# Order of weight preparation and evacuation at the start of both FFNs of a two-layer trunk

## The chip, the cores and the metric

The kernel runs on one core of a Trainium2 chip. The metric is the device time of one execution in microseconds (us). TensorE (PE in the profile, with PEld for its weight loads), VectorE (DVE), ScalarE (ACT) and GpSimd (POOL) each run their own queue in order; the sync engine (SP) issues most loads. An instruction that needs another engine's result waits for a semaphore, and everything behind it on its engine waits with it.

## The reference

Two layers, each a mixer with a residual and then a gated FFN with a residual, RMSNorm ahead of each, and a last RMSNorm. 512 tokens, 1024 channels, float32. The change is in the FFN, which stands once in each layer, with 2816 hidden channels:

```
def gated_conv_ffn(x, w_gate, w_up, conv_w, conv_b, w_down):
    g = jnp.einsum('bsd,df->bsf', x, w_gate)
    g = causal_dwconv3(g, conv_w) + conv_b
    up = jnp.einsum('bsd,df->bsf', x, w_up)
    return jnp.einsum('bsf,fd->bsd', jax.nn.silu(g) * up, w_down)
...
        hn = rms_norm(h, norm_ffn[layer])
        h = h + gated_conv_ffn(hn, w_ffn_gate[layer], w_ffn_up[layer], conv_ffn[layer],
                               b_conv_ffn[layer], w_ffn_down[layer])
```

## The kernel before, in words

Every float32 operand of a matmul is split into a high part (a rounded copy, made by ACT) and a low part (the rest, made by a DVE subtraction, or by an ACT copy with the sign turned and a GpSimd DMA that adds the original). A product is then three matmuls: high by high, high by low, low by high. Tiles named whi_ and wlo_ are the parts of weights, hgh and hgl those of the normalized input.

The 2816 hidden channels are 22 tiles of 128. `Ffn.steps` (L785) takes them in groups of two tiles, f = 0, 2, 4 and so on; in the text "group 2" is f = 2. For each group the gate (g) and up (u) projections are formed; then a `half_down` adds older groups' share of the down projection (PE rows named d in the first FFN and dn in the second), and `split_acts` splits the group's activations for it. A pool of 7 PSUM banks, "mm", carries all these products.

Group 0 is computed plainly by `direct` (L605), 96 matmuls of three passes into four banks gu_0 to gu_3. Its weights come from `pair_weights`. Its `evacuate` (L619) is the way out of the banks, for each of the two gate tiles: multiply by the norm's factor into a padded row (DVE, L624), convolve (`conv` L572: an ACT product, L575, then two DVE steps, L577, on a tile c), silu (ACT, L585, on a tile s, with a load of the function table ahead of the first), in the first FFN one more multiply by the norm's factor (DVE, L627), and then the product with the up bank (DVE, L630).

All later groups go through `both` (L682), a fast scheme with seven block products instead of eight for each of g and u. Its first half, up to L719, prepares weights: four loads of 512 KB into a pool of 4 raw tiles (`ffn_weights`, L547), the parts of the first blocks (tile a11), sums and differences of blocks on DVE (s12: L699, L701; s34: L710, L712), and their parts: whi_ on ACT and wlo_ on DVE (`halves`, L678), or for the blocks g and u themselves `summed` (L136: ACT L140, GpSimd DMA L141, ACT L143). Tiles of parts come from pools of 6 for each of high and low. Its second half runs the products in the order of the list at L745. Product numbers say which tiles take part: 1 uses a11, 5 and 6 use s12, 2 and 4 the blocks themselves, 7 and 3 use s34. Products 1, 6, 7 and 4 of one key add up in the same bank (PE rows g_2a, u_2a), 5 and 3 in another (g_2e, u_2e), 2 in a third (g_2b, u_2b). Between two products of a bank, ACT copies its state out (L733, to rows for g and to kept for u) or DVE adds it (L738, L743), so the next product of that bank waits for the copy.

The text's order is not the order on the engines. Except where `inorder` or `behind` pins an instruction, the framework's scheduler orders each engine's queue by its own estimate of readiness and by the order in which the text issues the instructions; tile buffers and semaphores follow from it. In the text before, the calls for groups 0 and 2 come in this order: direct products, block sums of the input (`block_sums`, L635), evacuation of group 0, preparation of group 2, products of group 2, half_down, split of the activations.

Of the kernel before, what the change touches and what calls it, by code (L numbers as in the profile page):

```python
# [32 lines left out]
def tile_trunk(ctx: ExitStack, tc: tile.TileContext, x, norm_mix, norm_ffn, final_norm,  # L33
# [50 lines left out]
    def behind(ins, first):  # L84

        if first is not None:
            tc.add_manual_dep(ins.ins, first.ins.name, mybir.DependencyInfo(
                mybir.DependencyClass.NoSync, mybir.DependencyReason.DATA), reason="order")
# [47 lines left out]
    def summed(raw, a, b, name, between=lambda: None):  # L136

        hi = wp.tile([P, a, b], F32R, tag="whi", bufs=6, name=f"whi_{name}")
        lo = wp.tile([P, a, b], F32R, tag="wlo", bufs=6, name=f"wlo_{name}")
        first = nc.scalar.activation(lo, raw, AF.Copy, scale=-1.0)  # L140
        nc.gpsimd.dma_start(lo, raw, accum_op=ALU.add)  # L141
        between()
        behind(nc.scalar.activation(hi, raw, AF.Copy), first)  # L143
        return hi, lo
# [138 lines left out]
    def padded_tile():  # L283
        turn[0] += 1
        return padded[turn[0] % NPADDED]
# [261 lines left out]
    def ffn_weights(layer, f, order):  # L547
        cs = slice(f * P, (f + 2) * P)
        return {(key, half): fetch(
            (w_ffn_gate if key == "g" else w_ffn_up)[layer][half * 512 : (half + 1) * 512, cs]  # L550
            .rearrange("(k p) c -> p k c", p=P), 4, 256, f"{key}{layer}_{f}_{half}")
            for key, half in order}

    class Ffn:
# [124 lines left out]
            nc.scalar.activation(hi, src, AF.Copy)  # L679
            nc.vector.tensor_tensor(lo, src, hi.bitcast(F32), ALU.subtract)  # L680

        def both(self, f):  # L682

            layer, ap, n = self.layer, self.ap, f"{self.layer}_{f}"
            raws = ffn_weights(layer, f, [(key, half) for half in range(2) for key in "gu"])
            stat = {}

            def put(key, product, hi_lo, i):
                stat[key, product] = hi_lo[0][:, i], hi_lo[1][:, i]

            w = self.unit(f"a11_{n}")
            for i, key in enumerate("gu"):
                self.halves(w[0][:, i], w[1][:, i], raws[key, 0][0][:, :, :P])
                put(key, 1, w, i)
            for key in "gu":
                r0, r1 = raws[key, 0][0], raws[key, 1][0]
                s12, s34 = (ap.tile([P, 2, 4, P], F32, tag="sum", bufs=3, name=f"{x}{key}_{n}")
                            for x in ("s12", "s34"))
                behind(nc.vector.tensor_tensor(s12[:, 0], r0[:, :, P:], r1[:, :, P:], ALU.add),  # L699
                       self.added[key])  # L700
                nc.vector.tensor_tensor(s12[:, 1], s12[:, 0], r0[:, :, :P], ALU.subtract)  # L701
                w = self.unit(f"s12{key}_{n}")

                def split_s12():
                    self.halves(*w, s12)

                hi, lo = summed(*raws[key, 1], between=split_s12)
                put(key, 5, w, 0)
                put(key, 6, w, 1)
                behind(nc.vector.tensor_tensor(s34[:, 0], r0[:, :, :P], r0[:, :, P:],  # L710
                                               ALU.subtract), self.added[key])
                nc.vector.tensor_tensor(s34[:, 1], r1[:, :, :P], s12[:, 1], ALU.subtract)  # L712
                for i, product in enumerate((2, 4)):
                    c = slice(i * P, (i + 1) * P)
                    stat[key, product] = hi[:, :, c], lo[:, :, c]
                w = self.unit(f"s34{key}_{n}")
                self.halves(*w, s34)
                put(key, 7, w, 0)
                put(key, 3, w, 1)  # L719

            banks = {"g": {}, "u": {}}
            kept = ap.tile([P, 3, HALF], F32, tag="kept", bufs=1, name=f"kept{n}")
            pads = [padded_tile() for _ in range(2)]
            lo, hi = slice(2, 2 + HALF), slice(2 + HALF, 2 + S)
            dst = {("g", 1): pads[0][:, lo], ("g", 6): pads[0][:, hi], ("g", 7): pads[1][:, hi],
                   ("g", 4): pads[1][:, lo]}
            dst.update({("u", product): kept[:, i, :] for i, product in enumerate((1, 6, 7))})
            onto = {2: 1, 5: 7, 3: 6}
            s, pending = {}, {}

            def after(key, product, ps):
                if (key, product) in dst:
                    nc.scalar.copy(dst[key, product], ps)  # L733
                elif product == 5 and (key, 7) not in pending:
                    pending[key, 5] = ps
                elif product in onto:
                    d = dst[key, onto[product]]
                    nc.vector.tensor_tensor(d, ps, d, ALU.add)  # L738
                if (key, product) == ("u", 4):
                    pending["u", 4] = ps  # L740
                if product == 7:
                    d = dst[key, 7]
                    self.added[key] = nc.vector.tensor_tensor(d, pending[key, 5], d, ALU.add)  # L743

            for key, product in (("g", 1), ("u", 1), ("g", 5), ("g", 6), ("u", 5), ("u", 6),  # L745
                                 ("g", 2), ("g", 7), ("u", 2), ("u", 7), ("g", 4), ("g", 3),
                                 ("u", 4), ("u", 3)):
                after(key, product, self.multiply(banks[key], f"{key}{n}", product,
                                                  stat[key, product]))
                if (key, product) in (("g", 4), ("g", 3)):  # L750
                    j = product == 4
                    row = pads[j][:, 2:]
                    nc.vector.tensor_tensor(row, row, self.r, ALU.mult)
                    s[j] = self.silu(self.conv(pads[j], f + j), f + j)
                    if j and layer == 0:
                        nc.vector.tensor_tensor(s[1], s[1], self.r, ALU.mult)
            nc.vector.tensor_tensor(s[1][:, HALF:], kept[:, 2, :], s[1][:, HALF:], ALU.mult)
            nc.vector.tensor_tensor(s[1][:, :HALF], pending["u", 4], s[1][:, :HALF], ALU.mult)
            if layer == 0:
                nc.vector.tensor_tensor(kept[:, :2, :], kept[:, :2, :],  # L760
                                        self.r.rearrange("p (a b) -> p a b", a=2), ALU.mult)
            s0 = s[0].rearrange("p (a b) -> p a b", a=2)
            nc.vector.tensor_tensor(s0, kept[:, :2, :], s0, ALU.mult)
            return [(f + 1, s[1]), (f, s[0])]

        def hidden(self, f, before=lambda i, j: None):

            if f == 0:
                def first(i, j):
                    before(i, j)  # L770
                    if (i, j) == (3, 0):
                        nc.vector.tensor_copy(self.cols, self.norm.rstd_cols(inorder))
                    elif (i, j) == (6, 0):
                        self.r = self.norm.rstd_spread(inorder)

                ch = self.pair_weights([("g", 0), ("u", 0), ("g", 1), ("u", 1)])
                rest = self.direct(ch, first)
                for kp in range(NP):
                    self.block_sums(kp)
                rows = rest()  # L780
            else:
                rows = self.both(f)
            return rows

        def steps(self, half_down, before=lambda i, j: None):  # L785

# [14 lines left out]
    def ffn0(norm):  # L801
        nonlocal prm1
        with tc.tile_pool(name="f0", bufs=1) as ap:
            def sums(kp):
                return [ap.tile([P, 2, HALF], F32R, name=f"t23{i}_{kp}") for i in "hl"]

            ffn = Ffn(0, prm0, norm, ap, sums)
            def half_down(a, b, half):
                project(f"d0_{a}", w_ffn_down[0], ffn.acts, list(range(a, b)), None,
                        halves=(half,), tail=0)  # L810

            ffn.split_acts(ffn.steps(half_down))
            prm1 = params1()
            nxt = Norm("m1", lambda k: prm1("mix", k))
            project("d0_last", w_ffn_down[0], ffn.acts, list(range(NF - 4, NF)), nxt)
            return nxt
# [370 lines left out]
    n = mixer0()  # L1187
    n = ffn0(n)
    n = mixer1(n)
# [31 lines left out]
```

## Time and profile before

| what | value |
|---|---|
| time before, median of 3 runs | 991.21 us (991.19 to 992.14) |
| the profiled execution's own time | 991.47 us |
| its span in the trace | 989.4 us |
| DVE busy | 770.3 us (78%) |
| ACT busy | 549.6 us (56%) |
| POOL busy | 101.0 us (10%) |
| read from memory | 98.42 MB, 102 GB/s over the span |
| granted TensorE clock | 0.999 of full speed |

How to read it: the trace starts all engines at the span's start. A row of the order of time gives the start, the length, the engine, the line of the kernel, the operation, the tiles written and read, and a count where equal rows follow each other. Brackets at the end hold the time that the engine had been idle and what ended that. Matmuls are pipelined: a matmul of 256 columns is shown 0.28 us long, while the next one starts 0.12 us after it, so an idle time in brackets is shorter than the delay of the start. On ACT and DVE, too, the next instruction starts a little before the shown end of the one before. The first FFN's products begin at 146.5 us and the second's at 632.6 us.

### The profile page before, as it was taken

To read this page: it belongs to the slowest core of one execution; us is meant where nothing else is said; L and a number is where in the kernel's file an instruction comes from. 1 tells how busy PE (TensorE), PEld (TensorE's weight loads), DVE (VectorE), ACT (ScalarE), POOL (GpSimd) and SP (SyncE) were. 2 spreads that over 40 slices of the span, in tenths; PEclk is the share of its full clock that TensorE was granted. 3 is DMA by queue.
4 is the path that set the end of the run, shared out by engine and by line. 5 is a ranking of instruction groups with operands and counts; after the bars stand their busy time and mean duration, and the time that the engine had idled before them with its cause. 6 is when DMAs were issued, how large, how long until landed. Compare 5 with 4: busy or idle time off the path is not lost.

```text
span 989.4 us, 15461 instructions
## 1 busy us (share of the span) xinstructions
PE 978.7 (99%) x6117; PEld 882.7 (89%) x6117; DVE 770.3 (78%) x1170; ACT 549.6 (56%) x823; POOL 101.0 (10%) x118
## 2 busy tenths in 40 slices
PE   9999999999999999999999999999999999999997
PEld 6788888899999999999889988889999999999986
DVE  5897458998788887886887665589987779777776
ACT  5623346765465654655487734676655456554544
POOL 2142022100000000000210001210000000000000
PEclk9999999999999999999999999999999999999999
DMA  7342225555455454553324623265555555455512
GB/s 247 131 149 85 86 86 128 131 143 153 129 149 133 131 142 129 150 129 110 124 64 116 199 74 102 54 139 129 150 162 134 131 148 146 118 136 135 143 49 85
DMA packets 86420, 125.64 MB, mean 127 GB/s; under 512 B 4196, under 2 KB 58188, under 8 KB 86348
## 3 DMA queue, kind: packets, MB, share of 16 engines
q1 hardware_dynamic: 77228, 98.24, 32.1%
q0 software_dynamic: 7200, 24.12, 13.4%
q10 hardware_dynamic: 1920, 2.30, 0.8%
q8 instruction: 48, 0.79, 0.3%
q14 instruction: 24, 0.20, 0.1%
HBM read 98.42 MB, written 2.10 MB: 102 GB/s over the span
## 4 chain that ended last, share of the span: by engine, by line
PE 85%; DVE 6%; ACT 3%; issue 1%; DMA 0%; ACTq 0%; POOL 0%; DVEq 0%
PE dn L154 4%; PE dn L155 4%; PE dn L156 4%; PE d L155 3%; PE d L154 3%; PE d L156 3%; PE oo L156 1%; PE oo L154 1%; PE oo L155 1%; PE oe L156 1%; PE oe L155 1%; PE oe L154 1%; PE u_20a L543 1%; PE u_18a L543 1%; PE u_16a L543 1%
## 5 line engine op out<-in xcount | busy, mean ns | idle before, releaser
L154 PE MATMUL dn<-whi_dn,a_hi 128*128 128x512 f32 (+1 forms) x180 | 69.3, 385 | 0.0
L155 PE MATMUL dn<-wlo_dn,a_hi 128*128 128x512 f32 (+1 forms) x180 | 69.3, 385 | 0.0
L156 PE MATMUL dn<-whi_dn,a_lo 128*128 128x512 f32 (+1 forms) x180 | 69.2, 384 | 0.0
L577 DVE SCALAR_TENSOR_TENSOR c<-rows,prm,c 128x512 f32<-128x512 f32 x88 | 63.8, 746 | 0.2 <-ACT c L575 0.2
L141 POOL DMA_DIRECT2D wlo_g<-raw_g x20 | 17.2, 861 | 385.2 <-ACT wlo_g L140 369.6
L154 PE MATMUL d<-a_hi,whi_d 128*128 128x512 f32 x144 | 56.1, 390 | 0.0
L155 PE MATMUL d<-a_lo,whi_d 128*128 128x512 f32 x144 | 56.1, 390 | 0.0
L156 PE MATMUL d<-a_hi,wlo_d 128*128 128x512 f32 x144 | 56.0, 389 | 0.0
L150 DVE TENSOR_TENSOR wlo_dn<-raw_dn,whi_dn 128x1024 fp32r<-128x1024 f32 x22 | 26.9, 1224 | 26.2 <-ACT whi_dn L149 26.0
L680 DVE TENSOR_TENSOR wlo_s34u<-s34u,whi_s34u 128x1024 fp32r<-128x1024 f32 x20 | 24.5, 1225 | 26.7 <-ACT whi_s34u L679 26.7
L1100 DVE SCALAR_TENSOR_TENSOR y<-dn,small,y 128x512 f32<-128x512 f32 (+1 forms) x49 | 33.9, 737 | 8.8 <-PE dn L156 8.8
L156 PEld LDWEIGHTS dn<-whi_dn,a_lo 128*128 128x128 f32 x180 | 33.8, 188 | 6.9 <-DVE a_lo L263 0.2
L154 PEld LDWEIGHTS dn<-whi_dn,a_hi 128*128 128x128 f32 x180 | 33.9, 188 | 6.5
L155 PEld LDWEIGHTS dn<-wlo_dn,a_hi 128*128 128x128 f32 x180 | 33.9, 188 | 6.3
L143 ACT ACTIVATE whi_u<-raw_u 128x1024 fp32r<-128x1024 f32 x21 | 22.1, 1055 | 30.0 <-PE d L155 16.3
L149 ACT ACTIVATE whi_dn<-raw_dn 128x1024 fp32r<-128x1024 f32 x22 | 23.3, 1059 | 25.5 <-issue 12.6
L261 ACT ACTIVATE a_hi<-s 128x512 fp32r<-128x512 f32 x44 | 27.4, 625 | 18.0 <-PE dn L155 12.3
L150 DVE TENSOR_TENSOR wlo_d<-raw_d,whi_d 128x1024 fp32r<-128x1024 f32 x18 | 22.0, 1224 | 19.7 <-ACT whi_d L149 19.7
L199 ACT ACTIVATE hgh<-h,prm 128x512 fp32r<-128x512 f32 x24 | 17.3, 723 | 35.1 <-DVE h L310 35.0
L585 ACT ACTIVATE s<-c,prm 128x512 f32<-128x512 f32 x44 | 31.2, 714 | 9.3 <-DVE c L577 9.3
L141 POOL DMA_DIRECT2D wlo_u<-raw_u x21 | 18.1, 862 | 166.4 <-ACT wlo_u L140 83.8
L210 POOL TENSOR_TENSOR ssq_f<-ssq_f,sq_f 128x512 f32<-128x512 f32 x14 | 19.8, 1412 | 131.2 <-ACT sq_f L209 96.3
(1435 smaller groups left out, 3664.0 us busy)
## 6 DMA issues: line engine op xcount, KB each, us to landing
raw_g<-in_w_ffn_gate_dram SPq DMA_DIRECT2D x40, 512.0 KB, 3.9
raw_u<-in_w_ffn_up_dram SPq DMA_DIRECT2D x40, 512.0 KB, 3.7
raw_dn<-in_w_ffn_down_dram SPq DMA_DIRECT2D x22, 512.0 KB, 3.6
wlo_u<-raw_u POOLq DMA_DIRECT2D x21, 512.0 KB, 5.6
wlo_g<-raw_g POOLq DMA_DIRECT2D x20, 512.0 KB, 4.7
raw_d<-in_w_ffn_down_dram SPq DMA_DIRECT2D x18, 512.0 KB, 3.7
raw_oe<-in_w_out_even_dram SPq DMA_DIRECT2D x8, 512.0 KB, 3.6
raw_v<-in_w_in_odd_dram SPq DMA_DIRECT2D x8, 512.0 KB, 4.6
```

The source lines that it names most:

```text
L141: nc.gpsimd.dma_start(lo, raw, accum_op=ALU.add)
L149: behind(nc.scalar.activation(hi, raw, AF.Copy), after[1])
L150: behind(nc.vector.tensor_tensor(lo, raw, hi.bitcast(F32), ALU.subtract), after[0])
L154: nc.tensor.matmul(ps, lhs[0], rhs[0], start=start, stop=False)
L155: nc.tensor.matmul(ps, lhs[0], rhs[1], start=False, stop=False)
L156: nc.tensor.matmul(ps, lhs[1], rhs[0], start=False, stop=stop)
L261: nc.scalar.activation(hi, src, AF.Copy, scale=scale)
L543: nc.tensor.matmul(ps, l, r, start=first, stop=end, skip_group_check=True)
L577: nc.vector.scalar_tensor_tensor(c, t[:, i : S + i], prm("cf", i * NF + ft), c, op0=ALU.mult, op1=ALU.add)
L585: nc.scalar.activation(s, c, AF.Silu, bias=self.prm("bf", ft))
L680: nc.vector.tensor_tensor(lo, src, hi.bitcast(F32), ALU.subtract)
L1100: nc.vector.scalar_tensor_tensor(dst, ps, ffn.cols[:, t : t + 1], dst, op0=ALU.mult, op1=ALU.add)
```

## The change

The method `both` is cut in two: `prepare`, which ends with the weight tiles in the dictionary `stat`, and `products`, which starts at the banks. For group 0 `hidden` now calls `prepare(2)` ahead of group 0's evacuation and keeps what it returns; for group 2 it uses that, and all later groups call both halves one after the other, as before. It applies to both layers' FFNs.

```diff
-        def both(self, f):
+        def prepare(self, f):
...
                 put(key, 7, w, 0)
                 put(key, 3, w, 1)
-
+            return stat
+
+        def products(self, f, stat):
+
+            layer, ap, n = self.layer, self.ap, f"{self.layer}_{f}"
             banks = {"g": {}, "u": {}}
...
                 for kp in range(NP):
                     self.block_sums(kp)
-                rows = rest()
-            else:
-                rows = self.both(f)
-            return rows
+                self.second = self.prepare(2)
+                return rest()
+            return self.products(f, self.second if f == 2 else self.prepare(f))
```

No instruction is added or left out; the text's order of the instructions named above is what differs, and with it the order that the scheduler gives them. Lines from L717 on are three or four further down in the changed kernel (L733 is L737 there, L738 is L742, L743 is L747).

## The prediction, made before the changed kernel ran

> **What bounds the kernel now.** First the page's head, then the busy time of the stretch between TensorE's first matmul (1.26 us) and its last (982.35 us):
>
> ```profile
> span 989.4 us, 15461 instructions
> PE 978.7 (99%) x6117; PEld 882.7 (89%) x6117; DVE 770.3 (78%) x1170; ACT 549.6 (56%) x823; POOL 101.0 (10%) x118
> ```
> ```profile
> 1.26:982.35 981.09, 978.74 (x6117) 882.71 (x6117) 767.54 (x1160) 548.23 (x819) 100.36 (x106) 1.00 0.47 128
> ```
>
> TensorE (PE) is busy 978.74 us of these 981.09: only 2.35 us can be won inside, and a little more where a matmul that had waited makes its follower late. The rest of the span (1.26 us ahead, 7.05 us behind) lies outside the change. So the second view is who PE waits for:
>
> ```profile
> PE u_2e L543 <- DVE wlo_s12u L680: 1.9, 2, 0.9
> PE g_2a L543 <- ACT rows L733: 0.2, 1, 0.2
> ```
>
> Nearly all of the 2.35 us is the second group (f = 2): two waits for the low part of the u sums (wlo_s12u), one in each FFN, and one for the copy of the first g product (rows, L733). The third view is PE's order of time there, in the first FFN and then in the second (start, length; in brackets the idle time before and what ended it):
>
> ```profile
> 174.00 0.40 PE L543 MATMUL u_2e<-t,whi_s12u 128*128 128x256 f32 x2
> 175.35 0.39 PE L543 MATMUL u_2e<-t,wlo_s12u 128*128 128x256 f32 x1 [0.95 <-DVE wlo_s12u L680]
> ...
> 177.37 0.28 PE L543 MATMUL g_2b<-hgh,whi_g 128*128 128x256 f32 x1
> 177.81 0.38 PE L543 MATMUL g_2a<-t23h,whi_s12g 128*128 128x256 f32 x1 [0.16 <-ACT rows L733]
> ...
> 663.37 0.40 PE L543 MATMUL u_2e<-t,whi_s12u 128*128 128x256 f32 x2
> 664.68 0.39 PE L543 MATMUL u_2e<-t,wlo_s12u 128*128 128x256 f32 x1 [0.91 <-DVE wlo_s12u L680]
> ...
> 668.01 0.28 PE L543 MATMUL u_2b<-hgh,wlo_u 128*128 128x256 f32 x1
> 668.17 0.50 PE L543 MATMUL g_2a<-t,whi_s12g 128*128 128x256 f32 x2
> ...
> 671.03 0.28 PE L543 MATMUL u_2a<-t,wlo_s12u 128*128 128x256 f32 x1
> 671.21 0.50 PE L543 MATMUL g_2a<-t,whi_s34g 128*128 128x256 f32 x2
> ```
>
> These matmuls start 0.12 us apart when nothing waits, and one that waited takes 0.10 more (0.38 or 0.39 for one, 0.50 for a pair, against 0.28 and 0.40), which its follower pays. First FFN: the wlo_s12u matmul was due at 174.24 and came at 175.35, 1.11 + 0.10; g_2a was due at 177.49 and came at 177.81, 0.32 + 0.10. Sum 1.63. Second FFN: due 663.61, came 664.68, 1.07 + 0.10; 668.13 against 668.17, 0.04 + 0.10; 671.15 against 671.21, 0.06 + 0.10. Sum 1.47. **3.10 us** is all that the change can win.
>
> Why were they late? ScalarE (ACT) and VectorE (DVE) in those microseconds:
>
> ```profile
> 169.39 1.06 ACT L679 ACTIVATE whi_s12u<-s12u 128x1024 fp32r<-128x1024 f32 x1 [1.48 <-DVE s12u L701]
> 170.66 1.34 ACT L575 ACTIVATE c<-rows,prm 128x512 f32<-128x512 f32 x2 [0.21 <-DVE rows L624]
> 171.91 1.04 ACT L140 ACTIVATE wlo_u<-raw_u 128x1024 fp32r<-128x1024 f32 x1
> 172.85 1.04 ACT L143 ACTIVATE whi_u<-raw_u 128x1024 fp32r<-128x1024 f32 x1
> 173.92 1.28 ACT L585 ACT_TABLE_LOAD   x1
> ...
> 177.40 0.35 ACT L733 COPY rows<-g_2a 128x256 f32<-128x256 f32 x1
> ...
> 659.04 1.06 ACT L679 ACTIVATE whi_s12u<-s12u 128x1024 fp32r<-128x1024 f32 x1 [1.95 <-PE gu L155]
> ```
> ```profile
> 169.94 1.28 DVE L624 TENSOR_TENSOR rows<-gu,rstd_f 128x512 f32<-128x512 f32 x2
> 171.42 2.74 DVE L577 SCALAR_TENSOR_TENSOR c<-rows,prm,c 128x512 f32<-128x512 f32 x4 [0.20 <-ACT c L575]
> 174.08 1.22 DVE L680 TENSOR_TENSOR wlo_s12u<-s12u,whi_s12u 128x1024 fp32r<-128x1024 f32 x1
> 175.97 1.30 DVE L627 TENSOR_TENSOR s<-s,rstd_f 128x512 f32<-128x512 f32 x2 [0.67 <-ACT s L585]
> ```
>
> wlo_s12u's input was whole at 170.45, but DVE first did the two rows of L624 and four steps of the first group's convolution (c, L577, 2.74 us) and began it at 174.08. The copy of g_2a, whose product ended at 171.28 (two products of 12 x 0.12 = 1.44 before 174.00, and 0.16 for the last to run out), stood on ACT behind c, a table load of 1.28 us, two silus and whi_s34u until 177.40.
>
> **The change part by part.** Nothing is added or removed: as many instructions on every engine, the same loads in the same order on the sync queue and on GpSimd's. And most of the preparation already stood ahead of the evacuation in the built order, since the scheduler does not follow the text. What moves, in both FFNs alike: on DVE wlo_s12u goes ahead of all four c steps and wlo_s34u ahead of the last; on ACT wlo_u and whi_u go ahead of c, and the first rows copy, whi_s34u and the first kept copy ahead of the table load and the silus; on PE the sixth product of g (g_2a, 12 matmuls) goes ahead of u_2e. In groups 4 and 6 of the first FFN three and two matmuls of g_4b and g_6b move in ahead of the wlo_s12u part of u_4e and u_6e.
>
> *Old waits.* First FFN, ACT walked on from whi_s12u at 169.39 with the spacing of the rows above (0.95 for a 1024-wide step, 1.25 for two c): wlo_u 170.34, whi_u 171.29, c 172.24 and 172.86, copy 173.49, over at 173.84 (0.35 long). Before, PE started 0.06 after the copy's end, so 173.90; PE is through with g_2e at 174.00. No wait, with 0.10 to spare. The copy has whi_s34u, the kept copy, the table load and both silus behind it on ACT, and itself waits for nothing there: g_2a is over at 171.28. wlo_s12u starts after the two L624 rows (171.2) and ends at 172.4; u_2e now comes one product later, at 175.44. No wait, 3 us to spare. So 1.63 goes.
>
> Second FFN: the same walk from 659.04 puts the copy at 663.11 to 663.46, PE at 663.52, while g_2e is through at 663.37: a new wait of 0.15 + 0.10 = 0.25. The others go. 1.47 - 0.25 = **1.22**.
>
> *What is late next.* PE is now early, DVE is not. DVE has the same list of work up to the next wlo_s12u, that of group 4, and is nearly full in the first FFN:
>
> ```profile
> 169.94:201.44 31.50, 30.39 (x230) 29.03 (x229) 30.38 (x49) 23.72 (x36) 2.57 (x3) 1.00 0.55 134
> 658.87:690.12 31.25, 30.34 (x228) 28.95 (x227) 28.98 (x46) 24.06 (x36) 2.59 (x3) 1.00 0.56 141
> ```
> ```profile
> 198.44 1.88 DVE L310 TENSOR_TENSOR h<-d,h 128x512 f32<-128x512 f32 x3
> ...
> 201.44 1.22 DVE L680 TENSOR_TENSOR wlo_s12u<-s12u,whi_s12u 128x1024 fp32r<-128x1024 f32 x1
> ...
> 690.12 1.23 DVE L680 TENSOR_TENSOR wlo_s12u<-s12u,whi_s12u 128x1024 fp32r<-128x1024 f32 x1
> ```
> ```profile
> 203.16 0.28 PE L543 MATMUL u_4e<-t,wlo_s12u 128*128 128x256 f32 x1
> ...
> 692.13 0.28 PE L543 MATMUL u_4e<-t,wlo_s12u 128*128 128x256 f32 x1
> ```
>
> (Windows: length, PE busy, PEld busy, DVE busy. Then DVE's adds of group 0's down products and its wlo_s12u of group 4 in each FFN, then PE's first matmul on that.) First FFN: DVE idles 31.50 - 30.38 = 1.12 us. Walked in the new order it waits about 0.6 for ACT's c (wlo_s12u over at 172.4, c ready at 172.95) and 0.2 for the first silu (table load after the kept copy, 174.95 to 176.25, silu to 177.0; DVE's last c over at 176.85). So DVE is 1.12 - 0.8 = 0.3 earlier; the bounds are 1.12 earlier (no idle left) and 2.44 later (both moved steps, 1.22 each, paid in full). I take 0.3, since the work is the same and only the idle time differs. wlo_s12u of group 4 is then over at 201.44 + 1.22 - 0.3 = 202.36, and PE (0.05 later, as at 175.30 to 175.35) may go at 202.41. PE wants it at 203.16 - 1.63 + 0.36 (three g_4b matmuls ahead) = 201.89. New wait 0.52 + 0.10 = 0.62. First FFN: 1.63 - 0.62 = **1.01**. Those three matmuls take the PSUM bank of the second down product, which the first of the three adds at 198.44 frees by 199.2, and weights whose low part GpSimd issues here and the page lets land 4.7 us later; both in time, and at nothing:
>
> ```profile
> 189.79 0.85 POOL L141 DMA_DIRECT2D wlo_g<-raw_g  x1 [15.69 <-DVE rows L738]
> ```
> ```profile
> wlo_g<-raw_g POOLq DMA_DIRECT2D x20, 512.0 KB, 4.7
> ```
>
> Second FFN: DVE idles 31.25 - 28.98 = 2.27, about 0.7 of which my walk gets back (0.75 for c, 0.35 for silu and some waits on ACT remain). PE wants 692.13 - 1.22 = 690.91; DVE needs to be 691.35 + 0.05 - 690.91 = 0.49 earlier. Just enough, no wait.
>
> Group 6 of the first FFN:
>
> ```profile
> 227.06 1.22 DVE L680 TENSOR_TENSOR wlo_s12u<-s12u,whi_s12u 128x1024 fp32r<-128x1024 f32 x1
> ```
> ```profile
> 228.66 0.28 PE L543 MATMUL u_6e<-t,wlo_s12u 128*128 128x256 f32 x1
> ```
>
> PE wants 228.66 - 1.01 + 0.36 (one more u_6a and two g_6b) = 228.01; DVE is over at 228.28 - 0.3 = 227.98 at the latest. No wait to speak of. From group 8 on each half_down has four tiles instead of two, and DVE is done with its backlog earlier, as in this stretch of group 8 (2.88 us busy of 5):
>
> ```profile
> 255.00:260.00 5.00, 5.00 (x44) 5.00 (x43) 2.88 (x3) 2.20 (x4) 0.00 (x0) 1.00 0.62 128
> ```
>
> So the lead stays to the end, and the 7.05 us behind the last matmul follow it.
>
> *Covered at no cost.* The silus, both products and the split acts of group 0 end about 1 us later, at about 182 in the walk; the first down matmul that reads them comes eleven products after 174.00, at 189.84, and u_2b's bank (freed by the first L630 step, about 179.0 in the walk) is wanted at 181.20, five products after it. Without that cover each 0.1 late is 0.1 on PE. GpSimd's wlo_u add starts 1.5 us earlier, which only helps.
>
> *A rule weighed.* That add's issue now falls beside wlo_s12u, a step with two SBUF inputs, rather than beside c. The trace has the pair elsewhere, both at their usual length:
>
> ```profile
> 679.08 1.22 DVE L680 TENSOR_TENSOR wlo_s12g<-s12g,whi_s12g 128x1024 fp32r<-128x1024 f32 x1
> ```
> ```profile
> 679.00 0.86 POOL L141 DMA_DIRECT2D wlo_g<-raw_g  x1 [15.56 <-ACT wlo_g L140]
> ```
>
> The Trainium skill, page "SBUF — State Buffer", section "Who interferes with whom", says that such a VectorE step contends with a GpSimd instruction that reads SBUF, and that the second one blocks fully. By these rows the issue is not such a reader, or reads too little to show. By the rule DVE's c would wait, and the sum would be 0.26 less.
>
> **Sum.** 1.01 + 1.22 = 2.23 us. 991.47 (this execution, its span of 989.4 and 2.07 around it) - 2.23 = 989.24; it lies 0.26 above the median of the runs, 991.21, so **989.0 us**, 0.23% faster.
>
> **The rivals.**
> (a) No new waits: all 3.10 go, 988.1. For it: DVE has more idle time than the 0.3 I take back. Against: before, DVE was done only 0.5 us ahead of PE at 203.16.
> (b) DVE is not earlier at all: in the first FFN it is ready for PE at 202.71 against 201.89, 0.92 lost of 1.63; in the second at 691.40 against 690.91, 0.59 lost of 1.22. 1.34 won, 989.9. For it: DVE idles 1.12 of 31.50 us, so a walk that is off by 0.3 decides.
> (c) DVE and GpSimd exclude each other: the issue (0.86) waits for wlo_s12u's end at 172.4 and holds c from 173.0 to 173.26. Then DVE's gain of 0.3 in the first FFN shrinks to 0.04 (in the second c comes no later than ACT lets it): 1.97 won, 989.2. Against it the pair at 679.
> (d) Slower: the moved steps push DVE back. Place: DVE between L624 and the next group's wlo_s12u. Each microsecond that DVE is late there comes off (b) twice. If both 1.22 were paid in full, 2 x 2.44 - 1.34 = 3.54 would be lost: 994.8. It decides from 0.67 us late in both FFNs, where won and lost cancel, and is past 0.2% from 1.66. Against it: the steps stood in this same stretch before, so only more idle time could do it.
> (e) The change does nothing, because the scheduler had done it already: excluded for the five steps named, whose order in the built program differs.
>
> **How the numbers follow.** A measurement of this kernel can tell about 0.2%, 2 us, from no change: 989.2 is the border. Forecast 0.60 (988.4 to 989.6, about four fifths of it under the border: 0.48), (a) 0.14, (b) and the cases between it and no change 0.14, (c) 0.04, (d) 0.08. Faster 0.48 + 0.14 = 0.62; within 0.12 + 0.14 + 0.04 = 0.30; slower 0.08. The range holds forecast, (a), (c) and (b) up to its value with a little for the spread of runs: 987.9 to 990.5, leaving out (d).
>
> **What would show it.** Right: PE's waits for wlo_s12u of group 2 are gone; the rows copy follows c on ACT at 173.5; a wait of about half a microsecond at u_4e in the first FFN only, and one of 0.1 to 0.2 at g_2a in the second; DVE's wlo_s12u of group 4 starts 0.3 earlier in the first FFN. Wrong: PE waits at u_4e or u_6e that together pass 1.6 us, u_2b waiting for its bank, or a GpSimd issue that lengthens.

## The result, and the profile after

The change made the kernel faster by about a quarter of a per cent: median 988.90 us of 12 runs (988.42 to 990.61) against 991.53 of 12 runs of before (991.01 to 992.14), ratio 0.9976, 95% interval 0.9969 to 0.9984. 989.0 had been forecast. The profiled execution took 989.93 us, span 988.2; it lies 1.0 above the median, and why is the first thing to find out. Who PE waits for, in us in total, times, and the longest:

```profile
PE u_0a L543 <- ACT u L941: 0.9, 1, 0.9
PE u_4e L543 <- DVE wlo_s12u L680: 0.3, 1, 0.3
```

The waits for wlo_s12u at u_2e and for rows at g_2a are gone, a short one at u_4e is new, and so is 0.9 us at u_0a, in the second layer's mixer, which the prediction did not have. Now PE in the order of time, in the first FFN (to 203) and the second:

```profile
174.00 0.28 PE L543 MATMUL g_2a<-t23h,whi_s12g 128*128 128x256 f32 x1
...
175.44 0.40 PE L543 MATMUL u_2e<-t,whi_s12u 128*128 128x256 f32 x2
...
201.78 0.28 PE L543 MATMUL g_4b<-hgh,wlo_g 128*128 128x256 f32 x1
202.34 0.39 PE L543 MATMUL u_4e<-t,wlo_s12u 128*128 128x256 f32 x1 [0.28 <-DVE wlo_s12u L680]
...
663.52 0.50 PE L543 MATMUL g_2a<-t,whi_s12g 128*128 128x256 f32 x2
...
690.91 0.28 PE L543 MATMUL u_4e<-t,wlo_s12u 128*128 128x256 f32 x1
```

Product 6 of g (g_2a) begins at 174.00 without a wait, u_2e follows at 175.44. The wlo_s12u matmul of u_4e was due at 201.90, 0.12 after its predecessor, and came at 202.34: 0.44 late, and 0.10 longer itself. In the second FFN g_2a comes at 663.52, where 663.37 had been its time, and u_4e at 690.91 waits for nothing. ACT and DVE over the same stretches:

```profile
172.24 1.32 ACT L575 ACTIVATE c<-rows,prm 128x512 f32<-128x512 f32 x2
173.47 0.35 ACT L737 COPY rows<-g_2a 128x256 f32<-128x256 f32 x1
...
174.68 0.36 ACT L737 COPY kept<-u_2a 128x256 f32<-128x256 f32 x1
175.14 1.28 ACT L585 ACT_TABLE_LOAD   x1
...
663.12 0.35 ACT L737 COPY rows<-g_2a 128x256 f32<-128x256 f32 x1
```
```profile
171.13 1.21 DVE L680 TENSOR_TENSOR wlo_s12u<-s12u,whi_s12u 128x1024 fp32r<-128x1024 f32 x1
172.98 2.08 DVE L577 SCALAR_TENSOR_TENSOR c<-rows,prm,c 128x512 f32<-128x512 f32 x3 [0.64 <-ACT c L575]
...
177.19 1.30 DVE L627 TENSOR_TENSOR s<-s,rstd_f 128x512 f32<-128x512 f32 x2 [0.33 <-ACT s L585]
...
201.07 1.21 DVE L680 TENSOR_TENSOR wlo_s12u<-s12u,whi_s12u 128x1024 fp32r<-128x1024 f32 x1
...
689.09 1.21 DVE L680 TENSOR_TENSOR wlo_s12u<-s12u,whi_s12u 128x1024 fp32r<-128x1024 f32 x1
```

On ACT both copies out of the banks now stand ahead of the table load (175.14). On DVE wlo_s12u ends at 172.34, and that of group 4 starts at 201.07, 0.37 earlier than the 201.44 of before; in the second FFN at 689.09 instead of 690.12.

Where did the profiled execution lose its lead? The program is cut at three matmuls that all kernels have: the first of group 2's products in the first FFN and in the second, and the program's last. Between the first two lies the mixer of the second layer. For before, for the changed kernel, and for a second profile of it (label "again" below), the rows of PE at these cuts, and from the mixer the issue of four loads of raw_u (SP), the DVE step that waits for the third of them, ACT's copy of u_0a and the matmul behind it:

```profile
169.69 0.28 PE L543 MATMUL g_2a<-hgh,whi_a 128*128 128x256 f32 x1
...
516.10 7.65 SPq L130 DMA_DIRECT2D raw_u<-in_w_in_odd_dram  x4
...
527.31 1.23 DVE L916 TENSOR_TENSOR raw_u<-raw_u,raw_u 128x1024 f32<-128x1024 f32 x1 [2.15 <-DMA raw_u<-in_w_in_odd_dram]
...
542.75 0.35 ACT L938 COPY u<-u_0a 128x256 f32<-128x256 f32 x1
...
543.15 0.39 PE L543 MATMUL u_0a<-whi_u,s 128*128 128x256 f32 x1
...
659.06 0.28 PE L543 MATMUL g_2a<-hgh,whi_a 128*128 128x256 f32 x1
...
982.07 0.28 PE L156 MATMUL dn<-whi_dn,a_lo 128*128 128x256 f32 x1
```
```profile
169.69 0.28 PE L543 MATMUL g_2a<-hgh,whi_a 128*128 128x256 f32 x1
...
515.00 7.65 SPq L130 DMA_DIRECT2D raw_u<-in_w_in_odd_dram  x4
...
527.51 1.23 DVE L919 TENSOR_TENSOR raw_u<-raw_u,raw_u 128x1024 f32<-128x1024 f32 x1 [3.46 <-DMA raw_u<-in_w_in_odd_dram]
...
542.72 0.35 ACT L941 COPY u<-u_0a 128x256 f32<-128x256 f32 x1
...
543.13 0.39 PE L543 MATMUL u_0a<-whi_u,s 128*128 128x256 f32 x1 [0.95 <-ACT u L941]
...
659.07 0.28 PE L543 MATMUL g_2a<-hgh,whi_a 128*128 128x256 f32 x1
...
980.86 0.28 PE L156 MATMUL dn<-whi_dn,a_lo 128*128 128x256 f32 x1
```
```profile
169.41 0.28 PE L543 MATMUL g_2a<-hgh,whi_a 128*128 128x256 f32 x1
...
514.75 7.65 SPq L130 DMA_DIRECT2D raw_u<-in_w_in_odd_dram  x4
...
526.02 1.23 DVE L919 TENSOR_TENSOR raw_u<-raw_u,raw_u 128x1024 f32<-128x1024 f32 x1 [2.22 <-DMA raw_u<-in_w_in_odd_dram]
...
541.39 0.35 ACT L941 COPY u<-u_0a 128x256 f32<-128x256 f32 x1
...
541.80 0.39 PE L543 MATMUL u_0a<-whi_u,s 128*128 128x256 f32 x1
...
657.73 0.28 PE L543 MATMUL g_2a<-hgh,whi_a 128*128 128x256 f32 x1
...
979.52 0.28 PE L156 MATMUL dn<-whi_dn,a_lo 128*128 128x256 f32 x1
```

First stretch: 659.06 - 169.69 = 489.37 us before, 489.38 in the first profile after, 488.32 in the second. Second stretch: 982.07 - 659.06 = 323.01 before, 321.79 and 321.79 after. So the second FFN gives 1.22 in both profiles; the first FFN gives 1.05 in one, and in the other the mixer took it back. The chain in the mixer can be read off: the loads were issued 1.1 us earlier after the change (515.00 against 516.10), but in the first profile the third came 12.51 us after the first issue, and in before and in the second profile 11.21 and 11.27. DVE's step waits for it, and ACT's copy of u_0a follows 15.2 to 15.4 us behind that in all three, with no slack: PE starts 0.40 or 0.41 after the copy does, every time. In before the load is only just what decides: ACT's copy of v_0a, for which ACT waits on PE's own products, ends at 528.46, and DVE is free for the next add at 528.50. So when the load is not late the chain follows PE, and a lead can pass through it.

### The profile page after: what moved, and what is told of

Same layout as the page of the kernel before. It is cut to its first block, busy times and chain, and to the rows that moved or that the text cites. A ratio compares the mean times of both kernels' runs of the same rounds, so it can differ in the third digit from the quotient of the medians.

```text
span 988.2 us, 15458 instructions
## 1 busy us (share of the span) xinstructions
PE 978.1 (99%) x6117; PEld 882.5 (89%) x6117; DVE 770.1 (78%) x1170; ACT 548.9 (56%) x823; POOL 100.1 (10%) x118
## 4 chain that ended last, share of the span: by engine, by line
PE 83%; DVE 8%; ACT 3%; issue 2%; DMA 1%; ACTq 0%; POOL 0%; DVEq 0%
PE dn L154 4%; PE dn L155 4%; PE dn L156 4%; PE d L155 3%; PE d L154 3%; PE d L156 3%; PE oo L156 1%; PE oo L154 1%; PE oo L155 1%; PE oe L156 1%; PE oe L154 1%; PE oe L155 1%; PE u_18a L543 1%; PE u_20a L543 1%; PE u_16a L543 1%
```

## The experiments

Each kernel is compared with runs of before beside it. The stretches are those of its one profiled execution; a star marks one with a u_0a wait of 0.3 us or more in it. Spans are medians over the runs; that of before is from the 33 runs beside the second profile, the two kernels with one FFN and VectorE's order, whose median was 991.40. The runs of before beside the others were a little longer: 991.65 (18 runs, span 989.65) beside c behind all preparation, late split, mixer's order and the first set of both edits, and 991.78 (21 runs, span 989.7) beside the rest.

| kernel | median us (runs) | ratio to before, 95% | span | stretch 1 | stretch 2 |
|---|---|---|---|---|---|
| before | 991.53 (12) | | 989.4 | 489.37 | 323.01 |
| changed | 988.90 (12) | 0.9976 (0.9969 to 0.9984) | 987.15 | 489.38* | 321.79 |
| changed, again | 988.89 (11) | 0.9976 (0.9967 to 0.9985) | 987.1 | 488.32 | 321.79 |
| first FFN only | 990.06 (11) | 0.9987 (0.9978 to 0.9996) | 988.3 | 488.29 | 322.99 |
| second FFN only | 990.33 (11) | 0.9990 (0.9982 to 0.9999) | 988.3 | 490.40* | 321.83 |
| VectorE's order only | 990.52 (11) | 0.9991 (0.9982 to 0.9999) | 988.8 | 489.02 | 322.80 |
| sums only | 991.49 (11) | 0.9995 (0.9986 to 1.0003) | 989.4 | 489.26 | 322.79 |
| c behind all preparation | 994.62 (9) | 1.003 (1.002 to 1.004) | 992.9 | 493.14* | 322.74 |
| late split | 988.90 (6) | 0.9972 (0.9960 to 0.9983) | 987.1 | 488.24* | 321.84 |
| mixer's order | 989.09 (9) | 0.9975 (0.9966 to 0.9985) | 987.0 | 488.27 | 321.83 |
| mixer's order, on before | 991.15 (11) | 0.9992 (0.9984 to 1.0001) | 989.3 | 489.30 | 322.98 |
| both edits | 988.06 (5) | 0.9962 (0.9950 to 0.9975) | 986.3 | 487.74 | 321.80 |
| both edits, again | 988.22 (5) | 0.9964 (0.9951 to 0.9978) | 986.5 | 487.79 | 321.79 |
| both and copy first | 987.89 (5) | 0.9961 (0.9949 to 0.9974) | 986.2 | 487.73 | 321.54 |

**The changed kernel again.** No edit.

> The changed kernel unchanged, a second profile and more runs. Theory (the lead of 1.1 us from the first FFN passes the mixer behind it in some executions and is lost there in others, at TensorE's wait for the copy of u_0a, behind a load of raw_u that lands at its own time): the runs again lie between 988.4 and 990.6, median 988.7 to 989.2; the profile shows either a u_0a wait of 0 to 0.3 us and a time near 988.7, or one of about 0.9 and a time near 989.9. Rival (the spread comes from elsewhere): the profile shows the u_0a wait of 0.9 to 1.0 whatever its time, or none beside a time near 989.9.

Median 988.89, runs from 988.61 to 989.73; the profiled one took 988.61 and shows no u_0a wait, as its rows above tell. The theory's pairing holds in both profiles: no wait with 988.61, the wait with 989.93.

**One FFN at a time.** In the text, for L = 0 or 1:

```diff
-                self.second = self.prepare(2)
-                return rest()
+                if self.layer == L:
+                    self.second = self.prepare(2)
+                    return rest()
+                rows = rest()
+                self.second = self.prepare(2)
+                return rows
```

> The change in the first FFN alone. Theory: old waits of 1.63 go, u_4e's new wait costs 0.5 to 0.6, so TensorE leaves the first FFN 1.1 us earlier; that lead then passes the mixer in some executions: median 990.2 to 990.9, 0.6 to 1.3 faster than before, runs spread over 1 us and more. Rival 1 (the mixer always takes the lead back): 991.3 to 991.6, no change, with a u_0a wait of 0.9 to 1.0. Rival 2 (the first FFN carries most of the measured 2.6): 989.6 or less.

> The change in the second FFN alone. Theory: 1.47 of waits go, 0.25 come back at g_2a, nothing stands behind that could take it back: 1.2 faster, median 990.1 to 990.5, runs as close together as before's (about 1 us). In the profile no u_0a wait in the mixer. Rival (the second FFN carries all of the measured 2.6 because the mixer takes back all of the first): 989.2 or less.

First FFN only: stretch 1 shorter by 1.08, stretch 2 as before; the lead passed the mixer, so rival 1 falls. Second FFN only: stretch 2 shorter by 1.18, stretch 1 not. The spans add up: 1.1 and 1.1 against 2.3 for the whole change, in its second set of runs beside the same 33 runs of before. But the second expectation was wrong in one point, and that is what taught most: this kernel has no lead in the mixer, and yet its profile shows the wait.

```profile
515.83 7.65 SPq L130 DMA_DIRECT2D raw_u<-in_w_in_odd_dram  x4
...
528.28 1.23 DVE L923 TENSOR_TENSOR raw_u<-raw_u,raw_u 128x1024 f32<-128x1024 f32 x1 [3.41 <-DMA raw_u<-in_w_in_odd_dram]
...
543.49 0.35 ACT L945 COPY u<-u_0a 128x256 f32<-128x256 f32 x1
...
543.90 0.39 PE L543 MATMUL u_0a<-whi_u,s 128*128 128x256 f32 x1 [0.89 <-ACT u L945]
```

12.45 us from the first issue to the step that needs the third load, then 15.21 to the copy: the load was late, and PE stood for 0.89 although it was not early. So the wait does not come from the change. It is a load whose time varies between executions, here by 1.3 us, ahead of a chain without slack. Its issue is not what varies: the third of the four goes out 6.1 to 6.2 us behind the first in all four profiles compared so far.

**VectorE's order only.** The kernel before with wlo_s12u ahead of the four c steps on DVE, and ACT's first rows copy held behind the silus. conv_steps are the c steps of group 0, first_silu its last silu:

```diff
+                    if (f, key) == (2, "u"):
+                        for step in self.conv_steps:
+                            behind(step, ins)
...
-                    nc.scalar.copy(dst[key, product], ps)
+                    ins = nc.scalar.copy(dst[key, product], ps)
+                    if (f, key, product) == (2, "g", 1):
+                        behind(ins, first_silu)
```

> The kernel before with wlo_s12u put ahead of the four c steps on VectorE, and ScalarE's first rows copy held behind both silus as it was. Theory (both halves of the move are needed, the copy on ScalarE as much as the low part on VectorE): u_2e's waits of 0.95 and 0.91 go, and TensorE waits about 1.4 us at g_2a for the rows copy in each FFN instead: 991.0 to 991.8, within 0.5 of before. Rival (VectorE's order alone carries the gain): no g_2a wait above 0.4, 989.0 to 989.6.

```profile
177.65 0.35 ACT L740 COPY rows<-g_2a 128x256 f32<-128x256 f32 x1
...
176.76 0.28 PE L543 MATMUL u_2a<-t23h,wlo_s12u 128*128 128x256 f32 x1
178.05 0.38 PE L543 MATMUL g_2a<-t23h,whi_s12g 128*128 128x256 f32 x1 [1.01 <-ACT rows L740]
```

The u_2e waits are gone and two waits at g_2a have come in their place: due at 176.88, started at 178.05 behind the rows copy of 177.65, 1.17 and 0.10 lost, with a like wait in the second FFN. It was smaller than the 1.4 expected, since the built order put product 6 of u in between, and the median, 990.52, came under the 991.0 to 991.8 expected. The two stretches gain 0.35 and 0.21, so 0.56 of the 2.3 is won. The rival falls: VectorE's order without ScalarE's first rows copy is worth a quarter of the change.

**Sums only.** `prepare` hands over to the evacuation behind wlo_s12u and wlo_u; whi_u and s34u come after it. Its main lines:

```diff
                 def split_s12():
                     self.halves(*w, s12)
+                    if key == "u":
+                        rows.extend(mid() or [])
...
-                self.second = self.prepare(2)
-                return rest()
+                self.second, rows = self.prepare(2, rest)
+                return rows
```

> Of the preparation only the parts up to the u sums (wlo_s12u, wlo_u) ahead of the evacuation, whi_u and the last difference (s34u) behind it, in both FFNs. ScalarE's c steps come 0.95 earlier, the copy stays at 173.5. Theory (what matters is wlo_s12u ahead of c and the copy ahead of the table load; VectorE's idle time between c and the silus sets u_4e): VectorE idles about 0.5 instead of 0.97 there, wlo_s12u of group 4 comes 0.4 to 0.5 earlier, is due 0.36 earlier, u_4e waits 0.3 to 0.5: 488.1 to 488.4 from the first to the second FFN's second group, median 988.5 to 989.2, the same as the changed kernel. Rival (s34u ahead is needed): a wait at the products of s34u, 989.3 or more.

```profile
177.14 0.35 ACT L739 COPY kept<-u_2a 128x256 f32<-128x256 f32 x1
...
176.56 0.28 PE L543 MATMUL u_2e<-t,wlo_s12u 128*128 128x256 f32 x1
177.54 0.38 PE L543 MATMUL u_2a<-t23h,whi_s12u 128*128 128x256 f32 x1 [0.70 <-ACT kept L739]
```

Missed: 991.49, no change that can be told. The rows copy came in time and u_4e did not wait (u_6e did, for 0.3), but the second copy, that of kept, fell behind the table load and the silus (177.14), and u_2a, due at 176.68, started at 177.54, with the same in the second FFN. The expectation had looked at one copy of two. So the gain hangs on at least three steps at once: wlo_s12u ahead of c, and the rows copy and the kept copy ahead of the table load. whi_s34u stood ahead of the table load in this kernel and in the one before it, so no run shows whether it has to.

**c behind all preparation.** All four c steps of group 0 held behind wlo_s34u (`self.low`, the last low part that the preparation makes):

```diff
+                if ft < 2:
+                    behind(ins, self.low)
```

> The changed kernel with all four c steps held behind wlo_s34u on VectorE, which then waits about 2 us for whi_s34u on ScalarE; behind that the built order also puts both s34u steps (0.60 each) ahead of wlo_s12u of group 4, and 16 matmuls of 0.12 ahead of u_4e's wlo_s12u part. Theory (VectorE's list up to the next wlo_s12u decides, as in the slow rival of the prediction): a u_4e wait of 1.5 to 2.5 us in the first FFN and some in the second, so that most of the gain is gone: 990.0 to 992.0. Rival (VectorE has enough idle time to take it): u_4e wait under 0.5 in both, 988.7 to 989.3.

```profile
174.78 1.23 DVE L683 TENSOR_TENSOR wlo_s34u<-s34u,whi_s34u 128x1024 fp32r<-128x1024 f32 x1 [2.47 <-ACT whi_s34u L682]
...
182.08 0.39 PE L543 MATMUL u_2b<-hgh,whi_u 128*128 128x256 f32 x1 [0.73 <-DVE s L633]
...
232.24 0.39 PE L543 MATMUL u_6e<-t,wlo_s12u 128*128 128x256 f32 x1 [1.06 <-DVE wlo_s12u L683]
```

The same four steps carried one further, and the kernel is slower than before: 994.62, above the 990 to 992 expected. DVE idles 2.47 us, and PE waits for it where the prediction had named a cover: at u_2b for the bank that the product of s with the up bank frees (0.73; L630 before, L633 in this kernel's lines), and at u_6e (1.06). Shorter waits come with them: 0.6 at u_4b for the DMA that completes wlo_u, 0.4 at g_4a for a rows copy. That u_4e would take most of it was wrong: it waits 0.2 in the first FFN and 0.6 in the second, both times for ACT's whi_s12u.

**Late split.** Group 2's activations are split only when group 4's rows are there, so that a_lo no longer stands ahead of wlo_s12u of group 4. One word in the table of steps:

```diff
-    STEPS = [(0, None, True), (2, (0, 2, 0), True), (4, (0, 2, 1), True)]
+    STEPS = [(0, None, True), (2, (0, 2, 0), False), (4, (0, 2, 1), True)]
```

> The changed kernel with the split of group 2's products (a_lo, two steps of 0.60 on VectorE) left until group 4's rows are there, so that it no longer stands ahead of wlo_s12u of group 4; u_4e is then due 0.36 earlier too, since three g_4b matmuls fall back behind it. Theory (VectorE's list alone makes the new u_4e wait): wlo_s12u of group 4 is over at 201.1 against a due time of 201.54, no u_4e wait, 0.5 faster than the changed kernel: median 988.2 to 988.6. Rival (u_4e waits for something else, or the wait comes back at u_6e): a wait of 0.2 or more at u_4e or u_6e, 988.8 to 989.1.

```profile
199.87 1.21 DVE L680 TENSOR_TENSOR wlo_s12u<-s12u,whi_s12u 128x1024 fp32r<-128x1024 f32 x1
...
201.30 0.28 PE L543 MATMUL u_4e<-t,wlo_s12u 128*128 128x256 f32 x1
...
542.03 0.39 PE L543 MATMUL u_0a<-whi_u,s 128*128 128x256 f32 x1 [0.36 <-ACT u L941]
```

wlo_s12u of group 4 is over at 201.08 and u_4e goes at 201.30 without a wait, as the theory has it, and u_6e does not wait. Yet the median did not move: 988.90, in the range of the rival, though not by the waits that it had named. The profile has a u_0a wait of 0.36 in its place: PE now comes to the mixer's copy another 0.54 earlier, and that chain had no slack left for it.

**The mixer's order.** The DVE step that waits for the load goes behind the first sum of v, and the scheduler then moved the copy of u_0a ahead of a table load (in the trace of the changed kernel with this edit, 540.10 and 540.74) and, on PE, that product of u_0a ahead of u_0e. So the edit takes the wait away by giving the copy slack; it does not make the load earlier:

```diff
-                    nc.vector.tensor_tensor(b12, b12, b11, ALU.subtract)
+                    behind(nc.vector.tensor_tensor(b12, b12, b11, ALU.subtract), first)
...
-            u0.rest()
+            u0.rest(v1.first_sum)
```

> The changed kernel with one step of the mixer, the difference of two raw_u tiles that waits for a load, put behind the first sum of v on VectorE. Theory (the load's landing time varies between executions, everything up to the copy of u_0a follows it, and this makes the runs of 989.3 to 990.6): no u_0a wait, and no run above 989.4; the median hardly moves, 988.6 to 989.0. Rival (the slower runs come from the start of the program, where z waits for hgh): the runs still reach 989.7 and more, with no u_0a wait in the profile.

> The mixer's order alone, on the kernel before. Theory (the load lands late in some executions of every kernel, and the copy of u_0a stands at the edge even in the profile of before): TensorE takes about 489.25 from the first to the second FFN's second group instead of 489.37, no u_0a wait, and the runs above 992 are gone; median 0.1 to 0.4 under before. Rival (the mixer matters only to a kernel that comes early): median within 0.1 of before and as wide a spread.

No u_0a wait in either. On the changed kernel it gave nothing by itself (0.05 in stretch 1). The expectation failed in one point: no run was to be above 989.4, and two were at 989.80 and 990.18, the sign that it had named for its rival, the start of the program where z waits for hgh. The traces show such a spread. In the 14 profiles the first matmul of z starts between 6.79 us (both edits, again) and 7.55 (first FFN only), and the first cut, where stretch 1 begins, comes 162.33 to 162.38 behind it in every one:

```profile
7.55 1.20 PE L420 MATMUL z<-hgh,whi_z 128*128 128x512 f32 x4 [1.32 <-ACT hgh L397]
```

hgh stands on ACT behind whi_z, which waits for a load of raw_z until 6.29 in this kernel and until 5.53 in the other. So 0.76 us of spread between executions is there before the FFN begins, and the stretches do not hold it. The two long runs themselves have no profile, so what made them stays open.

On before stretch 1 fell by 0.07, where 0.12 was expected; the median was 0.63 lower, but the interval holds no change, and one run was still at 992.12, where none above 992 was expected.

**Both edits.**

> Both of the last two edits on the changed kernel. Theory: no u_4e and no u_0a wait, the terms add: median 988.1 to 988.6, 2.8 to 3.3 faster than before, and runs within 1 us of each other. Rival (the lead is taken back somewhere behind): 988.8 to 989.1.

> The kernel with both edits (late split, order in the mixer) once more, for more runs. Theory (its gain over the changed kernel is u_4e's wait, which reaches the end only because the mixer's copy of u_0a no longer stops it): median 987.8 to 988.4 again; from the first FFN's second group to the second FFN's second group TensorE takes 487.6 to 487.9 us, against 488.3 in the undisturbed profile of the changed kernel. Rival (988.06 was luck of five runs): 988.6 to 989.0.

Stretch 1 is 487.74 and 487.79, 0.53 to 0.58 under the undisturbed profile of the changed kernel: u_4e's whole loss of 0.54, which the mixer no longer eats. Each edit alone left the median where it was (988.90 and 989.09, against 988.90 and 988.89). The intervals of the ratios are too wide to part both edits from the changed kernel; the stretch parts them, in two profiles, and nine of the ten runs lie under 988.42, the shortest of the changed kernel's 23.

**Copy first.** Both edits, and in the second FFN the rows copy of product 1 ahead of the two c steps on ACT (`ins` is that copy, `conv_starts` are the two c steps):

```diff
+                    if (layer, f, key, product) == (1, 2, "g", 1):
+                        for start in self.conv_starts:
+                            behind(start, ins)
```

> Both edits, and in the second FFN alone the first rows copy put ahead of the two c steps on ScalarE: it waits for nothing there and ends at about 0.35 after whi_u instead of 1.6. Theory (the new g_2a wait of the second FFN, 0.15 and 0.10 for the delayed matmul, is the time of those c steps): TensorE goes from u_2a to g_2a without a wait, the stretch from that group to the last matmul falls from 321.80 to 321.55, median 0.25 under the kernel with both edits. Rival (c, 0.25 later, makes VectorE late for u_4e in the second FFN): a u_4e wait there of 0.2 or more, nothing gained.

```profile
659.77 0.35 ACT L739 COPY rows<-g_2a 128x256 f32<-128x256 f32 x1
...
661.25 0.40 PE L543 MATMUL g_2a<-t,whi_s12g 128*128 128x256 f32 x2
```

The copy ends at 660.12, g_2a goes at 661.25 with no wait and in its usual 0.40, and stretch 2 is 321.54: 0.25 less, as forecast. With a median of 987.89 it is the fastest of all, though it cannot be told from the two before it by its runs (five each); by the stretches the three edits take 0.84 us more off than the change did in its second profile.

## Why the prediction was right, step by step

- **Old waits, 1.63 and 1.47:** gone in both FFNs.
- **ScalarE's walk:** the copy was put at 173.49 and 663.11 and came at 173.47 and 663.12; PE at 663.52, as written. The new wait of 0.25 in the second FFN was confirmed by taking it away.
- **wlo_s12u over at 172.4:** 172.34.
- **VectorE 0.3 earlier at group 4:** 0.37, but only partly for the reason given. The walk had idle time fall from 1.12 to 0.8. It fell to 1.00:

```profile
169.93:201.07 31.14, 31.14 (x241) 30.18 (x240) 30.14 (x50) 23.28 (x36) 2.56 (x3) 1.00 0.55 136
```

(31.14 us, DVE busy for 30.14 of them.) DVE waits 0.64 for c, where 0.6 was walked, and 0.33 for the first silu, where 0.2 was. The rest of the 0.37 is that the same list of steps covered 30.14 us instead of 30.38; why they overlapped more isn't shown.
- **New wait at u_4e, 0.62:** 0.54. First FFN 1.63 - 0.54 = 1.09 against 1.01 forecast; stretch 1 shows 1.05 and 1.08.
- **Second FFN, 1.22:** 1.22, with no wait at u_4e, which went at 690.91 as forecast; DVE was 1.03 earlier there, where 0.7 was claimed and 0.49 needed.
- **No wait at u_6e, and u_2b's bank in time:** right. What that cover is worth was seen when it was gone: 0.73 at u_2b and 1.06 at u_6e.
- **The rule weighed:** the GpSimd issue fell beside wlo_s12u,

```profile
171.69 0.86 POOL L141 DMA_DIRECT2D wlo_u<-raw_u  x1 [11.55 <-ACT wlo_u L140]
```

and both kept their length (0.86; 1.21 for the DVE step of 171.13), as in the pair at 679. So the 0.26 falls away. The prediction had applied the wrong rule: the Trainium skill, page "SBUF — State Buffer", section "Who interferes with whom", says that a tensor_tensor takes only the read side of the shared ports, while making a DMA's descriptors needs the write side, and marks this as inferred. The trace agrees with that. Nor was the pairing new: in before the issue stood at 173.25 beside c, which reads two SBUF tiles as well.
- **"So the lead stays to the end":** the weak step. Its ground was slack behind group 8; the mixer's load was not looked at. The median of the spans says that the lead usually stays; in the profiled execution 0.95 us of idle time came in at u_0a.
- **The sum, 2.23:** the spans fell from 989.4 in the 33 runs of before to 987.1 in the changed kernel's 11 runs beside them, by 2.3. The runs' own time fell by 2.63 in the first comparison and by 2.51 in that second one, since what lies around the span fell too, which the prediction had held fixed at 2.07 (below). That the time came within 0.1 of 989.0 is partly luck: the forecast started from 991.21, the median of three runs, where twelve gave 991.53, and its gain was 0.40 too small, and the two misses nearly cancel.
- **Rivals:** (a) and (b) are excluded by the u_4e wait, (c) by the POOL row. (d) was put at 994.8; the kernel that really pushes VectorE back took 994.62, but by other waits than its sum had, and all in stretch 1 (3.77 over before; stretch 2 lies 0.27 under it), where the sum had the loss in both FFNs, so the nearness of the figures is luck.

## What to carry to other kernels

When a scheduler orders the queues, a change in the text's order moves whole chains on several engines: list every copy and every add that must come ahead of the moved work, since a gain that hangs on three steps is gone when one falls behind a table load. Walk the new order from rows with the spacing they show; that gave starts 660 us into the program to 0.02 us. Then look for the next chain without slack (here a load, 15 us of two engines and a copy), because a lead ends there, and an edit whose gain cannot be seen alone can show it once the next chain has slack.

## What the runs showed that was not expected

The time around the span is a property of the built kernel, steady over its runs: device time less span was 2.04 us on average for before (2.00 to 2.09 in 33 runs), 1.77 after (1.73 to 1.82 in 12), 1.76 for the first FFN only, 2.05 for the second only and for the mixer's order, 1.73 with both edits. So 0.27 us of the measured gain lies outside what the profile shows, and no run tells why; kernels that differ by a few tenths are better compared by their spans.

The third raw_u load of the mixer was used 11.0 to 12.5 us after the first issue in the nine profiles with the mixer's order untouched, with the same loads in the same order (10.98 in VectorE's order only, 12.51 in the changed kernel). It is not alone in this: GpSimd's DMA for wlo_u, under way at the same time, landed 4.7 to 4.9 us after its issue in the five profiles where the load was used by 11.5, and 5.3 to 5.8 in the four where it was used later. The Trainium skill, page "DMA: Bandwidth & Descriptors", section "Latency and other measured facts", gives the memory's latency as 0.2 us on average and 2 us at high load, which would be room enough; no run here shows whether that is the cause.
